# Down projection: the last two k-tiles as a third pair of seven half-size products

## Chip, cores and metric

The kernel runs on one core of a Trainium2 chip. The metric is the device time of one execution in microseconds (us), the median of several runs. The profile is that of one execution.

## What is computed

One decoder layer on 512 tokens of width 1024, in fp32: an RMSNorm, a combined projection, two token mixers (block-sparse attention and a chunkwise mLSTM) merged by gates, an output projection, then the feed-forward block and a last norm. The change lies in the feed-forward block:

```python
u = rms_norm(h, norm_ffn_g[l])
g, up = jnp.split(u @ w_gate_up[l], 2, axis=-1)     # 1024 -> 2 x 2816
h = h + (jax.nn.silu(g) * up) @ w_down[l]           # 2816 -> 1024
...
return rms_norm(h, norm_final_g)
```

2816 is 22 k-tiles of 128 rows for the down projection.

## The kernel before

Every operand of a matmul is split into a high and a low part (ScalarE copies the high part into a rounded type, VectorE subtracts it for the low part), and a product is three passes: high x high, high x low, low x high. Most products are done by a scheme of seven half-size products in place of eight (W11, S1, S2, W12, S3, S4, W22): sums of halves of the weights and of the activations are formed first, and the seven results are added up with signs. S1 is W21+W22, S2 is S1+W11, S3 is W11+W21, S4 is S2+W12.

The feed-forward block has 22 gate/up items ("gu", one per k-tile of the down projection, each seven products of 128x256 matmuls, `prod`, L1120 to L1122), and five groups of the down projection ("ds"). A group takes four k-tiles as two pairs. Each of its seven products is done for two token tiles of 128, 512 columns wide, and adds up over the two pairs (`ds_prod`, L1378 to L1380: six matmuls). A pair's operands come from an even and an odd gate/up item: `gu_last` keeps the even one's results and combines them with the odd one's.

Groups 0 to 3 add their results to the stored residual by accumulating DMAs on GpSimd's queue (L1395). The last group, `ds_end`, adds to the residual in SBUF (tiles h, loaded by `end_load`, L1615; `add_`, L1462), squares it on ScalarE, forms the reciprocal root on two engines (`rstd`, L1474 to L1477, and `refine`, L1483 and L1484), scales by it and by the final norm's weights g3, and issues the output DMAs on SP's and ScalarE's queues.

5 x 4 k-tiles are 20 of the 22. Before, the last two are multiplied directly: `gu_last` splits their activations (L1341 to L1345), `dl_prep` splits their weights, 1024 columns each (`raw`, loaded at L1091), and `last` (L1508 to L1510) multiplies them in three passes, in banks that it shares with the seven products where it can: 48 matmuls in units of 512 columns.

The order of the work on an engine is set by a priority: `plan` gives each product a due time on a clock of TensorE's work, `at(key, product, offset)` sets the priority of what is issued next to such a time plus an offset, and a list scheduler issues the lowest that is ready. `behind` and `issue_after` add an order without a semaphore. Weights are split at due time minus H_OFF (high) and L_OFF (low), sums at minus S_OFF.

Elsewhere, and early in the kernel, four stores of rows (scr<-rr, L1762) and half of the loads of stacked keys (ks<-sd, L475) are issued on GpSimd's queue.

Of the kernel before, what the change touches and what calls it, by code (L numbers as in the profile page):

```python
# [15 lines left out]
P = 128  # L16
# [61 lines left out]
H_OFF, L_OFF, S_OFF, U_OFF, E_OFF, O_OFF, D_OFF, S4_OFF, R_OFF, RD_OFF = 1800, 800, 3800, 0, 3000, 1500, 1500, 10000, 1440, 1360  # L78

# [23 lines left out]
def hybrid_layer_kernel(ctx: ExitStack, tc, xw, xT, xtm, wall, wgt, wwo, wgu, wds, wdl, g3v, vecs, wgates, consts, rope, out):  # L103
# [349 lines left out]
    def rope_group(kind, g):  # L453
# [18 lines left out]
        for key, parts in lay:  # L472
            stk = slot4(F32R, key)
            for e, i in enumerate(parts):
                (nc.gpsimd if e % 2 else nc.sync).dma_start(  # L475
                    f(stk[32 * e : 32 * e + 32]), sd[i].rearrange("(h r) t -> r h t", h=4)
                )
            for j in range(4):
                stacks[(key, 4 * g + j)] = stk[:, j, :]
# [525 lines left out]
    def plan():  # L1005

        t = 0
        LONG = {"W12": 4, "LAST": 1, "W22": 4, "S4": 5}
        i0, i1, i2 = ITEMS[:3]
        seq = [(WO_ITEM, w) for w in WO_W] + [(i0, "W11"), (i0, "S1"), (i1, "W11"), (i1, "S1")]  # L1010
        seq += [(i, w) for i in (i0, i1) for w in ("S2", "S4", "S3")]
        seq += [(i0, "W12"), (i0, "W22"), (i2, "W11"), (i1, "W12"), (i1, "W22")]
        for j, x in enumerate(ITEMS):
            if j < 2:
                continue
            if j == len(ITEMS) - 1:
# [66 lines left out]
    def ds_load(n):  # L1083
        g = sw["ds", n] = {"w": {}}
        for j, k in enumerate(("W11", "W21", "W22", "W12")):
            g[k] = blk(name="raw", raw=True)
            nc.sync.dma_start(g[k], wds[n, j])
        if n == NG - 1:
            for k in range(LK):
                raw["dl", k] = blk(name="raw", raw=True)  # L1090
                nc.sync.dma_start(raw["dl", k], wdl[k])  # L1091

    DS_W = ("W11", "S1", "S2", "W12", "S3", "S4", "W22")

    def ds_prep(n):
# [3 lines left out]
        for k in DS_W if n < NG - 1 else DS_W[:3] + (0, 1) + DS_W[3:5] + DS_W[:4:-1]:  # L1099
            if k in (0, 1):  # L1100
                dl_prep(k)
                continue
            if k[0] == "S":
# [3 lines left out]
                V.tensor_tensor(g[k], g[a], g[b], op=ALU.add)  # L1107
# [4 lines left out]
            V.tensor_tensor(w[k][1], g[k], f(w[k][0]), op=ALU.subtract)
# [209 lines left out]
    hid = []  # L1322

    def gu_last(i):
# [14 lines left out]
        if i >= 4 * NG:  # L1339

            V.tensor_tensor(u[:, A_], u[:, A_], t[:, A_], op=ALU.mult)  # L1341
            V.scalar_tensor_tensor(u[:, B_], u[:, B_], -1.0, t[:, B_], op0=ALU.mult, op1=ALU.mult)
            h, l = slot(F32R, "ach"), slot(F32R, "acl")
            c = act_(h, u, AF.Copy)
            V.tensor_tensor(l, u, f(h), op=ALU.subtract)  # L1345
            hid.append((h, l))
            if i == FT - 1:
                ph["ins"].append(raw_ins(c))
        elif i % 2 == 0:
# [5 lines left out]
        else:  # L1355
# [10 lines left out]
            split_hl(e[:, A_], dst=(q[:, A_], q[:, B_]))  # L1366
# [4 lines left out]
    def ds_prod(ps, w, n, o, t, first=False):  # L1371

        wh, wl = w
        c = slice(t * P, (t + 1) * P)
        for k in range(2):
            bh, bl = (x[:, c] for x in hb[n][k][o])
            d = slice(k * S, (k + 1) * S)
            T.matmul(ps, bh, wh[:, d], start=first and k == 0, stop=False, skip_group_check=not first)  # L1378
            T.matmul(ps, bh, wl[:, d], start=False, stop=False, skip_group_check=not first)  # L1379
            T.matmul(ps, bl, wh[:, d], start=False, stop=k == 1, skip_group_check=not first)  # L1380

    LK = FT - 4 * NG
    DL = []

    def dl_prep(k):
        at(ITEMS[-1], "W12", -H_OFF)
        DL.append(split_hl(raw.pop(("dl", k)), dst=(blk(F32R, "w"), blk(F32R, "w"))))

# [57 lines left out]
    def ds_end():  # L1446
# [3 lines left out]
        key = ("ds", n)  # L1450
        w = sw.pop(key)["w"]
# [4 lines left out]
        U = 1360  # L1456
        v_ = lambda: small([P, 1], "v1")
# [29 lines left out]
        def apply(t, q, j):  # L1487

            V.scalar_tensor_tensor(hs[t][j], hs[t][j], q, g3[j], op0=ALU.mult, op1=ALU.mult)
            act_(hs[t][1 - j], hs[t][1 - j], AF.Copy, scale=q)  # L1490
            for e in (j, 1 - j):
                nc.sync.dma_start(out[t][:, e * S : e * S + S], hs[t][e])

        def scale_out(t, q, j):

            act_(hs[t][j], hs[t][j], AF.Copy, scale=q)
            nc.sync.dma_start(out[t][:, j * S : j * S + S], hs[t][j])

        def times_g(t, j):
            V.tensor_tensor(hs[t][j], hs[t][j], g3[j], op=ALU.mult)  # L1500

        def last(ps, t, j, first=False, d=slice(0, S)):

            q, c = slice(t * P, (t + 1) * P), slice(j * S + d.start, j * S + d.stop)
            for k in range(LK):
                (ah, al), (wh, wl) = hid[k], DL[k]
                g = dict(skip_group_check=not first)
                T.matmul(ps[:, d], ah[:, q], wh[:, c], start=first and k == 0, stop=False, **g)  # L1508
                T.matmul(ps[:, d], ah[:, q], wl[:, c], start=False, stop=False, **g)
                T.matmul(ps[:, d], al[:, q], wh[:, c], start=False, stop=k == LK - 1, **g)  # L1510
# [29 lines left out]
        for t in two:  # L1540
            at(key, "W22", U * t - 1000)
            add_(t + 2, 1, Z[t], r[t + 2])
        at(key, "LAST")
        y = accb()
        last(y, 2, 1, first=True)
        at(key, "W22", 2000)
        add_(2, 1, y, nr[2])
        square(2, 1)
        for t in two:
            at(key, "W22", 2 * U * t)  # L1550
            ds_prod(X[t], w["W22"], n, 6, t)
            last(X[t], t, 1)
            at(key, "W22", 2 * U * t + 1000)
            times_g(t, 0)
            at(key, "W22", 2 * U * (t + 1) + 200)
# [19 lines left out]
        with tc.issue_after(raw_ins(i[1])):
            apply(1, qs[1], 1)
        y = accb()
        lo, hi = slice(0, HS), slice(HS, S)
        at(key, "S4", 2 * U)
        ds_prod(Z[1], w["S4"], n, 3, 1)  # L1580
        last(Z[1], 3, 0)
        at(key, "S4", 4 * U + 200)
        add_(3, 0, Z[1], nr[3])
        square(3, 0)
        nc.gpsimd.tensor_tensor(hs[3][0], hs[3][0], g3[0], op=ALU.mult)
        at(key, "S4", 4 * U)
        last(y, 3, 1, first=True, d=lo)
        at(key, "S4", 9 * U // 2 + 200)
        add_(3, 1, y, nr[3], lo)
        square(3, 1, lo)  # L1590
        at(key, "S4", 9 * U // 2)
        y = mmb()
        last(y, 3, 1, first=True, d=hi)
        at(key, "S4", 5 * U + 200)
        add_(3, 1, y, nr[3], hi)
        square(3, 1, hi)
        q, v, i = rstd(3, "S4", 5 * U + 800)
        with tc.issue_after(raw_ins(i[1])):
            scale_out(2, qs[2], 0)
        q = refine(q, v)  # L1600
        for d in (lo, hi):
            act_(hs[3][0][:, d], hs[3][0][:, d], AF.Copy, scale=q)
            V.scalar_tensor_tensor(hs[3][1][:, d], hs[3][1][:, d], q, g3[1][:, d], op0=ALU.mult, op1=ALU.mult)
            nc.sync.dma_start(out[3][:, S + d.start : S + d.stop], hs[3][1][:, d])
        nc.scalar.dma_start(out[3][:, 0:S], hs[3][0])
# [130 lines left out]
    def gates():  # L1736
# [24 lines left out]
        for b in range(4):  # L1761
            nc.gpsimd.dma_start(scr[:, RS[b]], rr[b])  # L1762
# [440 lines left out]
```

## Time and profile before

| | |
|---|---|
| median of 3 runs | 722.72 us (722.56 to 723.15) |
| profiled execution | 722.84 us |
| its span | 721.1 us |
| granted TensorE clock | 0.998 |
| TensorE busy | 712.7 us, 99% of the span, 4310 matmuls |
| VectorE busy | 642.4 us, 89% |
| ScalarE busy | 467.0 us, 65% |
| GpSimd busy | 82.8 us, 11% |

The profile names engines PE (TensorE; PEld its weight loads), DVE (VectorE), ACT (ScalarE), POOL (GpSimd) and SP (the queue that issues most DMAs; SPq and ACTq rows are DMA issues). A group or timeline row reads: start, duration, engine, line, operation, out<-in, partitions x elements, count, and in brackets the engine's idle time before it and what ended it. Matmuls overlap in the pipeline, so a matmul's duration is longer than the time until the next one starts.

### The profile page before, as it was taken

Reading aid. Unit: us, or ns where it says so; the run is one execution under the profiler, and the core shown is the slowest. Engines: PE = TensorE matmul, PEld = TensorE weight load, DVE = VectorE, ACT = ScalarE, POOL = GpSimd, SP = SyncE. Lnnn points to the kernel's source line nnn. Section 1 sums busy time; section 2 is a strip of 40 time slices with the busy share of each in tenths; the row PEclk is TensorE's granted clock in tenths of the full one; section 3 lists DMA queues with packets and bytes.
Section 4 is the critical chain, followed back from the end, with each engine's and each line's share of the span. In section 5 each row is a group of like instructions: output and inputs, shape, how many; then the busy total and the mean of one; then the engine's idle time right before and its main releaser. Section 6 shows DMA issues by size and latency. Waiting matters only on the chain.

```text
span 721.1 us, 11772 instructions
## 1 busy us (share of the span) xinstructions
PE 712.7 (99%) x4310; PEld 636.8 (88%) x4310; DVE 642.4 (89%) x1125; ACT 467.0 (65%) x822; POOL 82.8 (11%) x105
## 2 busy tenths in 40 slices
PE   9999999999999999999999999999999999999995
PEld 6888888888888889998889998999899899899984
DVE  7998876899986698999999998899899899989996
ACT  7535777678776666965679666566565665655555
POOL 0004010102011010100000001300300310220000
PEclk9999999999999999999999999999999999999999
DMA  9778563858385967766797355974985795696403
GB/s 335 261 225 230 191 204 108 215 226 219 111 230 119 313 139 179 207 202 205 200 308 193 117 162 132 246 208 143 206 251 130 187 266 167 154 243 207 152 0 118
DMA packets 57418, 138.95 MB, mean 193 GB/s; under 512 B 5884, under 2 KB 10500, under 8 KB 57232
## 3 DMA queue, kind: packets, MB, share of 16 engines
q1 hardware_dynamic: 40448, 100.78, 40.9%
q0 software_dynamic: 15472, 34.92, 26.4%
q10 hardware_dynamic: 1440, 2.49, 0.9%
q8 instruction: 34, 0.56, 0.3%
q14 instruction: 24, 0.20, 0.1%
HBM read 121.35 MB, written 29.66 MB: 209 GB/s over the span
## 4 chain that ended last, share of the span: by engine, by line
PE 97%; ACT 1%; DVE 1%; issue 1%; DMA 0%
PE mm L234 9%; PE mm L235 9%; PE mm L236 9%; PE mm L1120 6%; PE mm L1121 6%; PE mm L1122 6%; PE s L1120 3%; PE s L1122 3%; PE s L1121 3%; PE mm L1378 3%; PE mm L1379 3%; PE mm L1380 3%; PE mm L329 2%; PE acc L1880 2%; PE mm L521 2%; PE mm L522 2%
## 5 line engine op out<-in xcount | busy, mean ns | idle before, releaser
L1120 PE MATMUL mm<-bq,w 128*128 128x256 f32 x264 | 75.2, 285 | 0.0
L1121 PE MATMUL mm<-bq,w 128*128 128x256 f32 x264 | 74.9, 284 | 0.0
L1122 PE MATMUL mm<-bq,w 128*128 128x256 f32 x264 | 74.7, 283 | 0.0
L166 ACT ACTIVATE w<-raw 128x1024 fp32r<-128x1024 f32 (+1 forms) x62 | 60.4, 983 | 13.6 <-PE mm L235 4.7
L166 ACT ACTIVATE w<-s 128x1024 fp32r<-128x1024 f32 (+1 forms) x54 | 55.4, 1026 | 14.2 <-DVE s L725 4.6
L179 DVE TENSOR_TENSOR wl<-raw,wh 128x1024 fp32r<-128x1024 f32 x42 | 50.8, 1220 | 11.2 <-ACT wh L166 7.8
L166 ACT ACTIVATE wh<-raw 128x1024 fp32r<-128x1024 f32 x42 | 44.2, 1057 | 25.4 <-PE mm L235 21.5
L1067 DVE TENSOR_TENSOR w<-s,w 128x1024 fp32r<-128x1024 f32 x42 | 51.2, 1219 | 7.1 <-ACT w L166 7.1
L1120 PEld LDWEIGHTS mm<-bq,w 128*128 128x128 f32 x264 | 50.5, 191 | 0.5 <-ACT s L166 0.3
L1121 PEld LDWEIGHTS mm<-bq,w 128*128 128x128 f32 x264 | 50.5, 191 | 0.0
L1122 PEld LDWEIGHTS mm<-bq,w 128*128 128x128 f32 x264 | 50.5, 191 | 0.0
L1120 PE MATMUL s<-bq,w 128*128 128x256 f32 x176 | 49.9, 284 | 0.0
L1121 PE MATMUL s<-bq,w 128*128 128x256 f32 x176 | 49.7, 283 | 0.0
L1122 PE MATMUL s<-bq,w 128*128 128x256 f32 x176 | 49.7, 283 | 0.0
L993 POOL DMA_DIRECT2D s<-in_wgu_dram x19 | 16.7, 879 | 231.2 <-DVE acl L179 93.5
L234 PE MATMUL mm<-u,wh 128*128 128x512 f32 x104 | 40.9, 393 | 0.0
L236 PE MATMUL mm<-u,wh 128*128 128x512 f32 x104 | 40.7, 391 | 0.0
L235 PE MATMUL mm<-u,wl 128*128 128x512 f32 x104 | 40.7, 391 | 0.0
L236 PE MATMUL mm<-ul,wh 128*128 128x512 f32 x104 | 40.5, 389 | 0.0
L234 PE MATMUL mm<-uh,wh 128*128 128x512 f32 x104 | 40.5, 389 | 0.0
L235 PE MATMUL mm<-uh,wl 128*128 128x512 f32 x104 | 40.5, 389 | 0.0
L166 ACT ACTIVATE s<-mm 128x256 f32<-128x256 f32 x44 | 16.7, 380 | 29.2 <-PE mm L1122 29.2
(499 smaller groups left out, 2438.2 us busy)
## 6 DMA issues: line engine op xcount, KB each, us to landing
raw<-in_wall_dram SPq DMA_DIRECT2D x42, 512.0 KB, 4.5
raw<-in_wgu_dram SPq DMA_DIRECT2D x22, 512.0 KB, 4.7
raw<-in_wds_dram SPq DMA_DIRECT2D x20, 512.0 KB, 6.2
s<-in_wgu_dram SPq DMA_DIRECT2D x19, 512.0 KB, 4.9
s<-in_wgu_dram POOLq DMA_DIRECT2D x19, 512.0 KB, 5.6
w<-in_wgu_dram SPq DMA_DIRECT2D x22, 256.0 KB, 5.6
ws<-in_wwo_dram POOLq DMA_DIRECT2D x8, 512.0 KB, 8.9
raw<-ws SPq DMA_DIRECT2D x8, 512.0 KB, 4.3
```

The costliest lines, as they stand in the source:

```text
L166: return A.activation(out_, in_, func, **kw)
L179: V.tensor_tensor(l, src, f(h), op=ALU.subtract)
L234: T.matmul(ps, wh[:, c], rh[j], start=start and j == 0, stop=False)
L235: T.matmul(ps, wl[:, c], rh[j], start=False, stop=False)
L236: i = T.matmul(ps, wh[:, c], rl[j], start=False, stop=stop and j == n - 1)
L1067: V.tensor_tensor(dst[1], src, f(dst[0]), op=ALU.subtract)
L1120: T.matmul(ps, wh[:, c], bh, start=first and k == 0, stop=False, skip_group_check=not first)
L1121: T.matmul(ps, wl[:, c], bh, start=False, stop=False, skip_group_check=not first)
L1122: i = T.matmul(ps, wh[:, c], bl, start=False, stop=k == 3, skip_group_check=not first)
L1378: T.matmul(ps, bh, wh[:, d], start=first and k == 0, stop=False, skip_group_check=not first)
L1379: T.matmul(ps, bh, wl[:, d], start=False, stop=False, skip_group_check=not first)
L1380: T.matmul(ps, bl, wh[:, d], start=False, stop=k == 1, skip_group_check=not first)
```

## The change

The last two k-tiles become a third pair of the last group. Items 20 and 21 go through the even and odd path that the others use. The weights of the pair are taken in halves of 512 columns: `end_first` splits W11, `end_second` forms S3, S1 and S2 and splits S1, `end_rest` splits the rest and forms S4. These four sums are on GpSimd, and so are the low parts of S3, W22 and S4 (`POOL_LO`). The sum and the low part of S4 of the first two pairs (1024 columns) go from VectorE to GpSimd as well.

In `ds_end` each product now adds up over three pairs (nine matmuls of 512 columns). S1 and S4 of the second token tile are issued in two halves of 256 columns, in banks of their own. `last`, `dl_prep`, `apply`, `scale_out` and `times_g` are gone. The multiplications by g3 of four tiles and the scalings of three tiles are on GpSimd, those of the other halves on VectorE and, for one, on ScalarE. The small tiles of the norm get buffers of their own.

One more edit is early in the kernel: the four stores scr<-rr are ordered after the last load of ks on GpSimd's queue.

The core of the diff:

```diff
-        for k in DS_W if n < NG - 1 else DS_W[:3] + (0, 1) + DS_W[3:5] + DS_W[:4:-1]:
-            if k in (0, 1):
-                dl_prep(k)
-                continue
+        for k in DS_W if n < NG - 1 else DS_W[:5] + DS_W[:4:-1]:
...
-                V.tensor_tensor(g[k], g[a], g[b], op=ALU.add)
+                pool(n, k).tensor_tensor(g[k], g[a], g[b], op=ALU.add)
...
+POOL_LO = ('S3', 'W22', 'S4')
+    pool = lambda n, k: nc.gpsimd if n == NG - 1 and k == 'S4' else V
+    def end_sum(s, a, b, dst):
+        at(ITEMS[-1], s, -SE_OFF)
+        end[s] = dst
+        nc.gpsimd.tensor_tensor(dst, end[a], end[b], op=ALU.add)
+    def end_split(k, h, l):
+        at(ITEMS[-1], k, -H_OFF)
+        act_(h, end[k], AF.Copy)
+        at(ITEMS[-1], k, -L_OFF)
+        (nc.gpsimd if k in POOL_LO else V).tensor_tensor(l, end[k], f(h), op=ALU.subtract)
+        sw[ITEMS[-1]]["w"][k].append((h, l))
...
-            hb[i // 4].append(ops + [(q[:, A_], q[:, B_])])
+            hb[min(i // 4, NG - 1)].append(ops + [(q[:, A_], q[:, B_])])
...
-        for k in range(2):
+        for k, (wh, wl) in enumerate(w):
...
+        def scale_p(t, q, j):
+            nc.gpsimd.tensor_scalar(hs[t][j], hs[t][j], q, None, op0=ALU.mult)
+            nc.sync.dma_start(out[t][:, j * S : j * S + S], hs[t][j])
...
-            last(y, t, 0, first=True)
-            ds_prod(y, w["W12"], n, 2, t)
+            ds_prod(y, w["W12"], n, 2, t, first=True)
...
+            nc.gpsimd.tensor_tensor(hs[t][0], hs[t][0], g3[0], op=ALU.mult)
...
-        for b in range(4):
-            nc.gpsimd.dma_start(scr[:, RS[b]], rr[b])
+        with tc.issue_after(marks["stack"]):
+            for b in range(4):
+                nc.gpsimd.dma_start(scr[:, RS[b]], rr[b])
```

What this moves, row by row. GpSimd's last rows before (s and c tiles are results of the group before; h is the residual, g the final norm's weights):

```order
L1395 DMA h1d<-c_7165 128x512
L993 DMA s_7203<-in_wgu_dram 128x1024
L1585 ISA
L1585 TENSOR_TENSOR h_7700<-h_7700,g_7692 128x512
```

and after (raw_7349 and raw_7351 are the two tiles of the third pair's weights, sw_7602, sw_7622 sums of the first two pairs' weights, v the factors of the norm):

```order
L998 DMA s_7203<-in_wgu_dram 128x1024
L1105 ISA
L1105 TENSOR_TENSOR sw_7859<-raw_7349 128x512
L1105 TENSOR_TENSOR raw_7349<-raw_7349,raw_7351 128x512
L1105 TENSOR_TENSOR raw_7349<-raw_7349 128x512
L1111 TENSOR_TENSOR w_7870<-sw_7859,w_7870 128x512
L1111 TENSOR_TENSOR w_7870<-raw_7351,w_7870 128x512
L1105 TENSOR_TENSOR raw_7351<-raw_7349,raw_7351 128x512
L1111 TENSOR_TENSOR w_7875<-raw_7351,w_7875 128x512
L1144 TENSOR_TENSOR sw_7622<-sw_7602,raw_7347 128x1024
L1150 TENSOR_TENSOR w_7625<-sw_7622,w_7624 128x1024
L1554 TENSOR_TENSOR h_7690<-h_7690,g_7688 128x512
```

Three more multiplications by g and three scalings follow. Nine operations on weights now stand ahead of the first multiplication by g, in the order in which their inputs come.

VectorE around the end of the last gate/up item, before (gt and up are its two results, acl the low part of the operand):

```order
L1337 TENSOR_TENSOR gt_7787<-mm_7712,rb_4349 128x256
L179 TENSOR_TENSOR w_7609<-raw_7349,w_7608 128x1024
L179 TENSOR_TENSOR w_7613<-raw_7351,w_7612 128x1024
L1341 TENSOR_TENSOR up_7802<-up_7802,gt_7787 128x256
L1342 SCALAR_TENSOR_TENSOR up_7802<-up_7802,gt_7787 128x256
L1112 TENSOR_TENSOR w_7617<-raw_7347,w_7616 128x1024
L1345 TENSOR_TENSOR acl_7848<-up_7802,ach_7847 128x512
```

and after:

```order
L1376 TENSOR_TENSOR gt_7784<-mm_7708,rb_4349 128x256
L1111 TENSOR_TENSOR w_7865<-raw_7349,w_7865 128x512
L1150 TENSOR_TENSOR w_7609<-raw_7347,w_7608 128x1024
L1387 SCALAR_TENSOR_TENSOR up_7799<-up_7799,gt_7784 128x256
L1388 TENSOR_TENSOR up_7799<-up_7799,gt_7784 128x256
L1390 TENSOR_TENSOR gt_7658<-gt_7658,up_7799 128x256
L1391 SCALAR_TENSOR_TENSOR gt_7658<-up_7799,up_7673 128x256
L1111 TENSOR_TENSOR w_7865<-raw_7351,w_7865 128x512
L182 TENSOR_TENSOR acl_7845<-up_7799,ach_7844 128x512
L1393 TENSOR_TENSOR up_7673<-up_7799,gt_7658 128x256
L182 TENSOR_TENSOR acl_7851<-gt_7658,ach_7850 128x512
```

Four operations of 256 columns and one more low part of 512 come in between the gate multiplication and the end of the operands; gt_7658 and up_7673 belong to item 20. The low part of 1024 columns that stays there is another's (W12).

On TensorE, where the third pair's operand acl_7851 is first read, after (product S2 of both token tiles; w_7865 holds the third pair's S2 weights, w_7604 and w_7605 those of the first two pairs):

```order
L1409 MATMUL mm_7879<-w_7865,ach_7850 128x512
L1410 MATMUL mm_7879<-w_7865,ach_7850 128x512
L1409 MATMUL mm_7880<-w_7604,ach_7315 128x512
L1411 MATMUL mm_7879<-w_7865,acl_7851 128x512
L1410 MATMUL mm_7880<-w_7605,ach_7315 128x512
```

In before S2 ran over two pairs only. Here the third pair closes it, and a matmul of the other token tile is issued ahead of the one that reads the low part.

More of the change, by code (lines that the diff above doesn't have):

```diff
@@ L1007, in plan @@
         t = 0
-        LONG = {"W12": 4, "LAST": 1, "W22": 4, "S4": 5}
         i0, i1, i2 = ITEMS[:3]
@@ L1016, in plan @@
             if j == len(ITEMS) - 1:
-                seq += [(x, w) for w in ("S1", "S2", "W12", "S3", "LAST", "W22", "S4")]
+                seq += [(x, w) for w in ("S1", "S2", "W12", "S3", "W22", "S4")]
                 continue
@@ L1088, in ds_load @@
         if n == NG - 1:
-            for k in range(LK):
+            for k in range(2):
                 raw["dl", k] = blk(name="raw", raw=True)
@@ L1093, in hybrid_layer_kernel, with end_first, end_second, end_rest @@
     DS_W = ("W11", "S1", "S2", "W12", "S3", "S4", "W22")
+    end = {}
+    pool = lambda n, k: nc.gpsimd if n == NG - 1 and k == 'S4' else V
[9 more added lines that the diff above has]
+        sw[ITEMS[-1]]["w"][k].append((h, l))
+    def end_first():
+        Lo, Hi = slice(0, S), slice(S, D)
+        d0, d1 = (raw.pop(("dl", i)) for i in range(2))
+        end.update(W11=d0[:, Lo], W21=d0[:, Hi], W12=d1[:, Lo], W22=d1[:, Hi])
+        end_split("W11", slot(F32R, "w"), slot(F32R, "w"))
+    def end_second():
+        t = slot4(F32R, "w")
+        end_sum("S3", "W11", "W21", slot4(name="sw")[:, 0, :])
+        end_sum("S1", "W21", "W22", end["W21"])
+        end_sum("S2", "S1", "W11", end["W11"])
+        end_split("S1", t[:, 0, :], t[:, 1, :])
+    def end_rest():
+        for i, k in enumerate(("S2", "W12", "S3", "W22", "S4")):
+            if i % 2 == 0:
+                t = slot4(F32R, "w")
+            if k == "S4":
+                end_sum("S4", "S2", "W12", end["W12"])
+            end_split(k, t[:, 2 * (i % 2), :], t[:, 2 * (i % 2) + 1, :])
     def ds_prep(n):
@@ L1338, in gu_last @@
         act_(t, t, AF.Silu)
[L1339 to L1349, printed above, removed]
+        if i % 2 == 0:
             at(key, "W22", O_OFF)
@@ L1365, in gu_last, with ds_prod @@
             q = slot(F32R, "ac")
-            split_hl(e[:, A_], dst=(q[:, A_], q[:, B_]))
+            c = act_(q[:, A_], e[:, A_], AF.Copy)
+            V.tensor_tensor(q[:, B_], e[:, A_], f(q[:, A_]), op=ALU.subtract)
+            if i == FT - 1:
+                ph["ins"].append(raw_ins(c))
             ops = [(p[0][:, c], p[1][:, c]) for p in (p0, p1, p2) for c in (A_, B_)]
-            hb[i // 4].append(ops + [(q[:, A_], q[:, B_])])
-    def ds_prod(ps, w, n, o, t, first=False):
-        wh, wl = w
+            hb[min(i // 4, NG - 1)].append(ops + [(q[:, A_], q[:, B_])])
+    def ds_prod(ps, w, n, o, t, first=False, d=slice(0, S)):
         c = slice(t * P, (t + 1) * P)
-        for k in range(2):
+        for k, (wh, wl) in enumerate(w):
             bh, bl = (x[:, c] for x in hb[n][k][o])
[L1377 to L1387, printed above, removed]
+            g = dict(skip_group_check=not first)
+            T.matmul(ps, bh, wh[:, d], start=first and k == 0, stop=False, **g)
+            T.matmul(ps, bh, wl[:, d], start=False, stop=False, **g)
+            T.matmul(ps, bl, wh[:, d], start=False, stop=k == len(w) - 1, **g)
     def ds_run(n):
@@ L1450, in ds_end @@
         key = ("ds", n)
+        marks["end0"], marks["end"] = st["S3"], st["W22"]
+        with behind("end0"):
+            end_second()
+        with behind("end"):
+            end_rest()
         w = sw.pop(key)["w"]
@@ L1455, in ds_end @@
         ss = {}
-        U = 1360
-        v_ = lambda: small([P, 1], "v1")
+        U = 2040
+        v_ = lambda: sm.tile([P, 1], F32, name=nm("v1"), tag="end", bufs=24)
         def add_(t, j, ps, c, d=slice(0, S)):
@@ L1485, in refine, with scale_g @@
             return r
-        def apply(t, q, j):
+        def scale_p(t, q, j):
+            nc.gpsimd.tensor_scalar(hs[t][j], hs[t][j], q, None, op0=ALU.mult)
+            nc.sync.dma_start(out[t][:, j * S : j * S + S], hs[t][j])
+        def scale_g(t, q, j):
             V.scalar_tensor_tensor(hs[t][j], hs[t][j], q, g3[j], op0=ALU.mult, op1=ALU.mult)
[L1490 to L1496, printed above, removed]
-            nc.sync.dma_start(out[t][:, j * S : j * S + S], hs[t][j])
[L1499 to L1510, printed above, removed]
+            nc.sync.dma_start(out[t][:, j * S : j * S + S], hs[t][j])
         qs = []
         X, Z = [mmb() for t in two], [sb() for t in two]
+        lo, hi = slice(0, HS), slice(HS, S)
+        zh = sb()
         for t in two:
@@ L1541, in ds_end @@
             at(key, "W22", U * t - 1000)
[L1542 to L1548, printed above, removed]
+            for z, d in ((Z[t], slice(0, S)),) if t == 0 else ((Z[t], lo), (zh, hi)):
+                add_(t + 2, 1, z, r[t + 2], d)
+            square(t + 2, 1)
+            nc.gpsimd.tensor_tensor(hs[t + 2][1], hs[t + 2][1], g3[1], op=ALU.mult)
         for t in two:
-            at(key, "W22", 2 * U * t)
+            at(key, "W22", U * t)
@@ L1551, in ds_end @@
             ds_prod(X[t], w["W22"], n, 6, t)
[L1552 to L1555, printed above, removed]
+            at(key, "W22", U * (t + 1) + 200)
             add_(t, 1, X[t], r[t])
             square(t, 1)
-            q, v, _ = rstd(t, "W22", 2 * U * (t + 1) + 2000)
+            q, v, i = rstd(t, "W22", U * (t + 1) + 1600)
             qs.append(refine(q, v))
-            if t == 0:
-                apply(0, qs[0], 1)
+            scale_p(t, qs[t], 0)
@@ L1575, in ds_end @@
[L1575 to L1599, printed above, removed]
+        at(key, "S4", U)
+        ds_prod(Z[1][:, lo], w["S4"], n, 3, 1, d=lo)
+        at(key, "S4", 3 * U // 2 + 200)
+        add_(3, 0, Z[1], nr[3], lo)
@@ L1600, in ds_end @@
+        square(3, 0, lo)
+        at(key, "S4", 3 * U // 2)
+        ds_prod(zh[:, hi], w["S4"], n, 3, 1, d=hi)
+        at(key, "S4", 2 * U + 200)
+        add_(3, 0, zh, nr[3], hi)
+        square(3, 0, hi)
+        at(key, "S4", 2 * U + 400)
+        scale_p(2, qs[2], 1)
+        q, v, i = rstd(3, "S4", 2 * U + 800)
+        with tc.issue_after(raw_ins(i[0])):
+            scale_g(2, qs[2], 0)
         q = refine(q, v)
         for d in (lo, hi):
-            act_(hs[3][0][:, d], hs[3][0][:, d], AF.Copy, scale=q)
```

46 lines of the change are left out of this document (26 added, 20 removed).

## The prediction, made before the result was known

> **What bounds the kernel now.** I read the page's busy shares and its chain first, then the windows of the last 80 us, then the timelines of TensorE, VectorE and the queues at the end.
>
> ```profile
> PE 712.7 (99%) x4310; PEld 636.8 (88%) x4310; DVE 642.4 (89%) x1125; ACT 467.0 (65%) x822; POOL 82.8 (11%) x105
> PE 97%; ACT 1%; DVE 1%; issue 1%; DMA 0%
> ```
>
> The first row gives busy time per engine, the second the chain that ended last: TensorE is nearly the whole of it. The windows (columns: PE, PEld, DVE, ACT and POOL busy, granted clock, DMA share, GB/s) place that in the stretch of the change:
>
> ```profile
> 660.00:680.00 20.00, 20.00 (x158) 19.35 (x156) 18.50 (x32) 11.42 (x19) 0.00 (x0) 1.00 0.54 185
> 680.00:700.00 20.00, 20.00 (x111) 17.37 (x111) 18.76 (x25) 11.28 (x17) 0.00 (x0) 1.00 0.00 1
> 700.00:722.00 22.00, 13.85 (x67) 11.43 (x65) 15.11 (x36) 10.82 (x29) 1.26 (x1) 0.93 0.26 96
> ```
>
> PE is busy all 20 us of both windows, so a matmul less is time less. VectorE is second, at 18.5 and 18.8 of 20: it has 1.2 to 1.5 us to spare per window. GpSimd does nothing there.
>
> TensorE's timeline gives the matmul prices (start, duration, engine, line):
>
> ```profile
> 677.52 0.40 PE L1378 MATMUL mm<-w,ach 128*128 128x512 f32 x1
> ...
> 686.58 0.40 PE L1379 MATMUL s<-w,ach 128*128 128x512 f32 x1
> ...
> 712.26 0.28 PE L1508 MATMUL acc<-w,ach 128*128 128x256 f32 x1
> ...
> 713.58 0.28 PE L1510 MATMUL mm<-w,acl 128*128 128x256 f32 x1
> ```
>
> Durations overlap, so I price by starts. From 686.58 to 712.26 lie 113 matmuls of 512 columns: 25.68/113 = 0.227 us each. From 712.26 to 713.58 lie 11 steps of 256 columns: 0.12 each. The last one starts at 713.58; the span ends at 721.1, 7.5 us later, and the profiled run took 722.84, 1.74 us more than its span. That run is 0.12 above the median of 722.72.
>
> **The change: TensorE.** From 677.52, the first product of the last group, before issues 126 matmuls of 512 columns (84 of the seven products, 42 of the direct ones), 12 of 256 at the end, and 48 of 256 of the last gate/up item: 126 x 0.2273 + 60 x 0.12 = 35.84; the rows give 713.70 - 677.52 = 36.18, so some 0.3 us are gaps. After: 7 products x 2 token tiles x 9 matmuls = 126 in units of 512, of which the second tiles of S1 and S4 (18) are issued as 36 halves. That is 108 x 0.2273 + 36 x 0.12 + 48 x 0.12 = 34.63. Gain 1.2 us: 6 matmuls saved are 1.36, the extra halving costs 0.15. The matmuls would end at about 712.5.
>
> **VectorE, where the slack is none.** The third pair needs the two activations combined and split, more work than before. Its prices:
>
> ```profile
> 675.93 1.23 DVE L1112 TENSOR_TENSOR w<-raw,w 128x1024 fp32r<-128x1024 f32 x1 [0.55 <-ACT w L166]
> ...
> 686.81 0.42 DVE L1337 TENSOR_TENSOR gt<-mm,rb 128x256 f32<-128x256 f32 x1
> 687.14 2.35 DVE L179 TENSOR_TENSOR w<-raw,w 128x1024 fp32r<-128x1024 f32 x2
> 689.41 0.42 DVE L1341 TENSOR_TENSOR up<-up,gt 128x256 f32<-128x256 f32 x1
> 689.75 0.42 DVE L1342 SCALAR_TENSOR_TENSOR up<-up,gt 128x256 f32<-128x256 f32 x1
> 690.08 1.22 DVE L1112 TENSOR_TENSOR w<-raw,w 128x1024 fp32r<-128x1024 f32 x1
> 691.22 0.68 DVE L1345 TENSOR_TENSOR acl<-up,ach 128x512 fp32r<-128x512 f32 x1
> 691.82 1.40 DVE L1462 SCALAR_TENSOR_TENSOR h<-mm,nrc,h 128x512 f32<-128x512 f32 x2
> 693.14 1.22 DVE L1107 TENSOR_TENSOR sw<-raw,raw 128x1024 f32<-128x1024 f32 x1
> ```
>
> From start to start: 256 columns 0.34, 512 columns 0.60, 1024 columns 1.14, a 512 addition from PSUM 0.66. In after, the last gate/up item's W22 ends 19 matmuls of 512 and 49 of 256 past 677.52, at 688.0 (before: 13 and 48). The gate multiplication then starts 0.25 later, as it did before; up to the low part of the third pair's operand for S2 (acl_7851) VectorE runs six 256 steps, four 512 and one 1024: 6 x 0.34 + 4 x 0.60 + 1.14 = 5.6, so it lands at about 693.9. TensorE reaches the first matmul that reads it 17 of 512 and 17 of 256 after W22, 5.9 us, at 693.9. Zero slack. The other tight point is the low half of the first product's weights (w_7593), ready in before at 677.07 (675.93 + 1.14) for 677.52; the added sum and operand work of item 20 ahead of it delays it by about 0.6. I allow 0 to 0.4 for both, and take 0.1.
>
> **GpSimd.** Four sums and three low parts of 512, one sum and one low part of 1024, four multiplications by g3 and three scalings of 512 are put on it. Its only price in the trace:
>
> ```profile
> 664.48 6.54 SPq L1091 DMA_DIRECT2D raw<-in_wdl_dram  x2
> ...
> 714.15 1.26 POOL L1585 TENSOR_TENSOR h<-h,g 128x512 f32<-128x512 f32 x1 [64.53 <-ACT sq L166]
> raw<-in_wdl_dram SPq DMA_DIRECT2D x2, 512.0 KB, 3.8
> ```
>
> 1.26 for 512, twice VectorE's 0.60; 1024 columns are 2.5 by doubling. Between 672 and 702 that is 7 x 1.26 + 2 x 2.5 = 13.8 us in 30: room enough. The raw weights are issued by 671.0 and landed by 674.8; S3, S1 and S2 need 3.8 us in turn from about 672 and are due on TensorE after 689. The first sum waits for the landing, and all of GpSimd's rows stand behind it, the longest string last: the S4 sum of the third pair, then the sum and low part of pairs 0 and 1 (2.5 each), ScalarE between them: done by 701.5, TensorE reads S4 at about 708, slack 6 us. GpSimd's own speed is thus covered; what is not covered is what it does to VectorE (rival B). Moving this work off VectorE also takes two 1024 operations (2.3 us) and one 512 multiplication from it before 711.
>
> **The tail.**
>
> ```profile
> 713.89 0.48 DVE L1462 SCALAR_TENSOR_TENSOR h<-mm,nrc,h 128x256 f32<-128x256 f32 x1 [0.19 <-PE mm L1510]
> 714.50 0.21 DVE L1474 TENSOR_SCALAR v<-v,v 128x1 f32<-128x1 f32 x1
> 715.01 0.21 DVE L1477 TENSOR_SCALAR v<-v,v 128x1 f32<-128x1 f32 x1 [0.30 <-ACT sq L166]
> ...
> 716.03 0.88 DVE L1603 SCALAR_TENSOR_TENSOR h<-h,v,g 128x256 f32<-128x256 f32 x2
> 715.45 1.54 ACT L166 ACTIVATE h<-h,v 128x512 f32<-128x512 f32 x3
> 717.02 0.36 ACTq L1605 DMA_DIRECT2D out_dram<-h  x1
> 716.61 0.88 SPq L1604 DMA_DIRECT2D out_dram<-h  x2
> out_dram<-h SPq DMA_DIRECT2D x2, 128.0 KB, 2.4
> ```
>
> From the last matmul's start to the last output issue (about 717.1) 3.5 us pass, then 4.0 to the span's end. The form stays: last half added, squared, root, refined, scaled in halves by VectorE and ScalarE, three issues. New is the queue of outputs: SP now also holds the tile that GpSimd scales last (h_7695). Its factor is ready at about 713.2; its scaling is a one-input form that the trace doesn't have, between VectorE's 0.60 and GpSimd's 1.26. I take 1.26, the row of its own engine: 714.5. The last row's scaling comes at 714.8, so the queue isn't held. The tail keeps its 7.5 us, give or take 0.2. The Trainium skill, "GPSIMD Engine Reference", section 4.1, says that one-input operations run at about line rate there: an estimate of 0.6 by that, with the output free at 713.8 and no case left for rival C below; no run here shows it.
>
> **The early edit.** Two pairs of ks loads now go ahead of the first of the four scr stores on GpSimd's queue:
>
> ```profile
> 54.76 0.54 POOL L1762 DMA_DIRECT2D scr<-rr  x1 [7.93 <-DVE rr L1757]
> 55.28 2.18 POOL L475 DMA_DIRECT2D ks<-sd  x4
> 57.45 0.53 POOL L1762 DMA_DIRECT2D scr<-rr  x1
> ...
> 64.64 0.39 PE L523 MATMUL acc<-wh,ul 128*128 128x512 f32 x1
> 64.86 0.22 PE L1788 MATMUL s<-ks,qs 128*128 128x128 f32 x1
> ```
>
> The loads start 0.5 us sooner, the first store 2.2 later. TensorE reached ks at 64.86 without a gap (0.22 after its last start), so nothing is won; the other stores are not issued before 57.45 either. Zero, bounds -0.3 and +0.3 (a store's 0.5 either way).
>
> **Sum.** -1.2 (matmuls) + 0.1 (tight points) + 0 (tail, GpSimd, early edit) = -1.1 to -1.2. Against the run's 722.84 that is 721.65; against the median, 721.5. The bound of faster and slower is 0.2%, 1.45 us, which this gain just misses.
>
> **Rivals.** A is the above, with VectorE undisturbed.
>
> B, slower: GpSimd and VectorE hold each other up when both read two SBUF tiles. In before GpSimd's one operation ran from 714.15 to 715.41 beside a PSUM addition (0.48, like others) and 128x1 operations, so nothing excludes it. Place: 688 to 694, where VectorE has no slack and GpSimd does the low parts of S3 and W22 and the S4 sum, 1.26 each. If VectorE stops for two or three, TensorE waits 2.5 to 3.8 for acl_7851; the sums from 672 on do the same ahead of w_7593, worth 0.7 to 1.8 beyond its slack. With -1.2 from the matmuls: +1.3 to +4.4, middle +2.3, 725.0. It decides from 1.2 us of VectorE standing still in that stretch, one operation. For it: VectorE is at 94%. Against it: some operations there are PSUM additions, and GpSimd may come second and be the one that waits, with 6 us to spare. The Trainium skill, "SBUF — State Buffer", section "Who interferes with whom", states such a rule: a VectorE instruction with two SBUF inputs contends with a GpSimd instruction that reads SBUF, and the second to issue fully blocks. By it B would be the forecast; no run here shows it yet.
>
> C: the gain is given back at the output queue. If GpSimd's scalings and multiplications are late by more than 0.3 us (the space between 714.5 and 714.8), SP's issues stand behind h_7695, in order. One more 1.26 in GpSimd's row costs 1.0: 722.5, no change.
>
> **Chances.** A 0.53: it holds at -1.2 plus or minus 0.7 (the tight points, the tail, the early edit), so 0.25 of it is beyond 1.45, where VectorE's relief also closes the gaps, and 0.28 within. B 0.35: 0.32 slower, 0.03 within. C 0.12: 0.11 within, 0.01 slower. Faster 0.25, same 0.42, slower 0.33. The range leaves out A's best (0.07) and the worse part of B (0.12): 720.7 to 725.5; the likeliest case alone is 720.8 to 722.2.
>
> **What would show it.** Right: PE without idle time from 677 to the end, the last matmul starting 1.2 us earlier, VectorE's 1024 operations still 1.14 apart while POOL works, the last output issue at about 715.9. B shows as longer VectorE rows beside POOL rows and a PE gap of over 1 us at the third pair's S2 or at the first product. C shows as an SP issue of h_7695 after the last row's scaling. I am wrong if PE ends earlier and the span doesn't, or if another stretch than this one moves by over 0.5 us.

## The result, and the profile after

The changed kernel takes 730.78 us (median of 4 runs, 730.52 to 731.48); before, run beside it, 722.87. The ratio is 1.0111, 95% interval 1.0094 to 1.0129: 8 us slower, outside the predicted range.

The page of the changed kernel (busy time, and the chain that ended last):

```profile
PE 712.9 (98%) x4316; PEld 635.7 (87%) x4316; DVE 650.7 (89%) x1127; ACT 467.3 (64%) x825; POOL 108.2 (15%) x120
PE 91%; DVE 5%; issue 2%; ACT 1%; DMA 1%; SPq 0%; DVEq 0%; ACTq 0%
```

VectorE is busy 8.3 us longer in all, TensorE is no longer busy throughout, and VectorE has 5% of the chain. The windows place it (PE, PEld, DVE, ACT, POOL busy, clock, DMA share, GB/s):

```profile
660.00:680.00 20.00, 18.64 (x154) 18.33 (x152) 19.25 (x29) 10.77 (x17) 4.54 (x3) 1.00 0.52 176
680.00:700.00 20.00, 17.02 (x104) 14.26 (x102) 19.48 (x29) 10.62 (x19) 4.94 (x4) 1.00 0.02 9
700.00:720.00 20.00, 18.49 (x86) 14.97 (x87) 18.58 (x27) 10.24 (x22) 13.56 (x9) 1.00 0.01 1
```

TensorE idles 1.4, 3.0 and 1.5 us where it idled nothing. TensorE's waits of over 1 us from 650 us on (engine and line, what it waited for, us in total, times, longest):

```profile
PE mm L1411 <- DVE acl L182: 1.5, 1, 1.5
PE mm L1409 <- ACT sq L169: 1.5, 1, 1.5
PE mm L1161 <- DVE gt L1351: 1.4, 1, 1.4
PE mm L1409 <- ACT ach L169: 1.2, 1, 1.2
```

The first row is the operand that the prediction found without slack. For the second the view names ScalarE's squaring of the residual, which itself follows VectorE's additions; the matmul also waits for its bank, which the VectorE addition from 711.30 to 712.03 empties. The third is item 20's W22, which waits for its bank until VectorE has emptied it at 677.16 (L1351); that operation stands behind the first two rows below. What VectorE did there, and GpSimd at the same time, from their timelines:

```profile
673.43 1.78 DVE L182 TENSOR_TENSOR acl<-gt,ach 128x512 fp32r<-128x512 f32 x1
675.13 1.51 DVE L1396 TENSOR_TENSOR ac<-up,ac 128x256 fp32r<-128x256 f32 x1
...
693.03 1.51 DVE L1387 SCALAR_TENSOR_TENSOR up<-up,gt 128x256 f32<-128x256 f32 x1
694.46 1.51 DVE L1388 TENSOR_TENSOR up<-up,gt 128x256 f32<-128x256 f32 x1
695.89 0.41 DVE L1390 TENSOR_TENSOR gt<-gt,up 128x256 f32<-128x256 f32 x1
...
697.76 1.49 DVE L1393 TENSOR_TENSOR up<-up,gt 128x256 f32<-128x256 f32 x1
...
702.01 2.63 DVE L1396 TENSOR_TENSOR ac<-up,ac 128x256 fp32r<-128x256 f32 x1
...
707.02 3.04 DVE L1150 TENSOR_TENSOR w<-raw,w 128x1024 fp32r<-128x1024 f32 x1
```

```profile
675.01 1.35 POOL L1105 TENSOR_TENSOR raw<-raw,raw 128x512 f32<-128x512 f32 x1 [0.35 <-DMA raw<-in_wdl_dram]
...
692.64 1.62 POOL L1111 TENSOR_TENSOR w<-sw,w 128x512 fp32r<-128x512 f32 x1 [13.97 <-ACT w L169]
694.21 1.47 POOL L1111 TENSOR_TENSOR w<-raw,w 128x512 fp32r<-128x512 f32 x1
...
697.37 1.60 POOL L1105 TENSOR_TENSOR raw<-raw,raw 128x512 f32<-128x512 f32 x1 [1.69 <-issue]
...
701.42 2.93 POOL L1144 TENSOR_TENSOR sw<-sw,raw 128x1024 f32<-128x1024 f32 x1 [0.42 <-PE mm L1410]
706.58 2.40 POOL L1150 TENSOR_TENSOR w<-sw,w 128x1024 fp32r<-128x1024 f32 x1 [2.22 <-DVE w L1150]
```

Read them side by side. The 256-column operations at 693.03 and 694.46 take 1.51 where the one at 695.89 takes 0.41: GpSimd's low parts run from 692.64 to 695.68. The one at 702.01 takes 2.63, beside GpSimd's 1024 sum; the low part at 707.02 takes 3.04 where before it took 1.22, beside GpSimd's. The one at 697.76, ahead of the operand that TensorE waits for, takes 1.49 beside the sum at 697.37. Each is longer by 1.1 beside a 512 operation and by 1.8 to 2.2 beside one of 1024.

The ends tell how long the hold lasts. VectorE's 256-column operations end 0.28 or 0.29 us after GpSimd's operation beside them (676.64 after 676.36, 694.54 after 694.26, 695.97 after 695.68, 699.25 after 698.97, 704.64 after 704.35), the one of 1024 ends 1.08 after it (710.06 after 708.98). That is a little less than such operations take from start to start (0.34 and 1.14). So in these rows VectorE gets through its data only when GpSimd has finished, and the hold is what GpSimd's operation still has to run.

TensorE's steps, and its last matmul (before: 713.58, with 7.5 us to the span's end):

```profile
677.63 0.39 PE L1161 MATMUL mm<-bq,w 128*128 128x256 f32 x1 [1.36 <-DVE gt L1351]
...
695.78 0.39 PE L1411 MATMUL mm<-w,acl 128*128 128x512 f32 x1
697.41 0.50 PE L1409 MATMUL mm<-w,ach 128*128 128x512 f32 x1 [1.25 <-ACT ach L169]
...
697.98 0.40 PE L1409 MATMUL mm<-w,ach 128*128 128x512 f32 x1
699.91 0.50 PE L1411 MATMUL mm<-w,acl 128*128 128x512 f32 x1 [1.53 <-DVE acl L182]
...
710.29 0.39 PE L1411 MATMUL mm<-w,acl 128*128 128x512 f32 x1
712.18 0.47 PE L1409 MATMUL mm<-w,ac 128*128 128x512 f32 x1 [1.51 <-ACT sq L169]
...
720.45 0.28 PE L1411 MATMUL s<-w,acl 128*128 128x256 f32 x1
```

Around 697, 700 and 712 three steps lose 1.40, 1.70 and 1.66 us against a step of 0.23. The end, on GpSimd, VectorE and SP:

```profile
722.10 2.05 POOL L1518 TENSOR_SCALAR h<-h,v 128x512 f32<-128x512 f32 x1 [0.67 <-DVE v L1503]
```

```profile
723.51 0.88 DVE L1600 SCALAR_TENSOR_TENSOR h<-h,v,g 128x256 f32<-128x256 f32 x2
```

```profile
724.17 0.33 SPq L1519 DMA_DIRECT2D out_dram<-h  x1
724.60 0.38 SPq L1524 DMA_DIRECT2D out_dram<-h  x1
725.07 1.51 SPq L1602 DMA_DIRECT2D out_dram<-h  x2
```

GpSimd's scaling takes 2.05, not 1.26. SP issues that tile at 724.17, another behind it, and the last row's two halves, scaled at 723.95 and 724.39, only from 725.07.

The 8.6 us between the two spans (the profiled execution of the changed kernel is the slowest of its four) can be split by marks that both traces have. The first mark is the SiLU of item 19, in before and after:

```profile
666.90 0.64 ACT L171 ACTIVATE gt<-gt 128x512 f32<-128x512 f32 x1 [1.63 <-DVE gt L1337]
```

```profile
667.64 0.64 ACT L174 ACTIVATE gt<-gt 128x512 f32<-128x512 f32 x1 [1.63 <-DVE gt L1376]
```

0.74 lies before it, in a part that the change does not touch but for the early edit, which is taken up below (in the twelve profiles of the layer here this mark stands between 666.67 and 667.64). From there to the last matmul's start it is 46.68 before and 52.81 after: 6.13. The tail is 7.52 and 9.25: 1.73. Of the 6.13, the matmuls that are saved give back 1.2, so that waits cost 7.3: 1.6 ahead of the last group's first product (679.88, 12.24 after the mark; before 10.62), most of it the 1.36 of item 20's W22; 0.4 at that product's second matmul, for the low half of its weights; 4.8 in the three steps above; the rest, 0.6, in small ones.

### The profile page after: what moved, and what is told of

Its sections match the earlier page's. It is cut to its first block, busy times and chain, and to the rows that moved or that the text cites. A ratio compares the mean times of both kernels' runs of the same rounds, so it can differ in the third digit from the quotient of the medians.

```text
span 729.7 us, 11822 instructions
## 1 busy us (share of the span) xinstructions
PE 712.9 (98%) x4316; PEld 635.7 (87%) x4316; DVE 650.7 (89%) x1127; ACT 467.3 (64%) x825; POOL 108.2 (15%) x120
## 4 chain that ended last, share of the span: by engine, by line
PE 91%; DVE 5%; issue 2%; ACT 1%; DMA 1%; SPq 0%; DVEq 0%; ACTq 0%
PE mm L237 9%; PE mm L238 8%; PE mm L239 8%; PE mm L1161 5%; PE mm L1162 5%; PE mm L1163 5%; PE s L1163 3%; PE s L1161 3%; PE s L1162 3%; PE mm L1410 2%; PE mm L1409 2%; PE mm L1411 2%; PE acc L1879 2%; PE mm L527 2%; PE mm L526 2%
```

## The experiments

The two measures of each profile are T, from item 19's SiLU to the last matmul's start, and E, from there to the span's end; they are from one execution of each kernel. Each ratio is to runs of before beside it (medians 722.87 to 723.35).

| kernel | time, us | ratio to before, 95% | T | E |
|---|---|---|---|---|
| before | 722.87 | | 46.68 | 7.52 |
| changed | 730.78 | 1.0094 to 1.0129 | 52.81 | 9.25 |
| e1 fills in place of arithmetic on weights | 723.67 | 0.9999 to 1.0018 | 45.56 | 9.23 |
| e2 weights on VectorE | 728.18 | 1.0052 to 1.0082 | 48.33 | 10.69 |
| e3 tail off GpSimd | 731.62 | 1.0105 to 1.0139 | 53.85 | 8.02 |
| e5 sums by DMA, rest on VectorE | 725.41 | 1.0022 to 1.0047 | 46.68 | 9.83 |
| e6 nothing on GpSimd | 726.67 | 1.0037 to 1.0064 | 47.92 | 9.58 |
| e7 fills, tail off GpSimd | 722.59 | 0.9985 to 1.0003 | 45.60 | 8.00 |
| e8 early edit alone | 723.33 | 0.9995 to 1.0013 | 46.68 | 7.54 |
| e9 e5 with the first additions by DMA | 722.54 | 0.9985 to 1.0003 | 45.77 | 7.90 |
| e10 two low parts on VectorE | 729.96 | 1.0084 to 1.0115 | 50.37 | 10.26 |
| e12 e9 with its tail reordered | 723.83 | 0.9996 to 1.0014 | 45.73 | 8.69 |

**e1, fills.** The theory after the result is the prediction's rival B, a hold of VectorE by GpSimd; its rival L is that VectorE's own work is too long.

```diff
-        nc.gpsimd.tensor_tensor(dst, end[a], end[b], op=ALU.add)
+        nc.gpsimd.memset(dst, 0.5)
...
-        (nc.gpsimd if k in POOL_LO else V).tensor_tensor(l, end[k], f(h), op=ALU.subtract)
+        if k in POOL_LO:
+            nc.gpsimd.memset(f(l), 0.0)
```

> The changed kernel with the nine operations of GpSimd on weights (four sums, three low parts, the sum and the low part of the first pairs' S4) replaced by fills of a constant into the same tiles: they write and read nothing, so these products are computed from constants. VectorE's work is unchanged. Theory B (a GpSimd operation that reads SBUF stops VectorE's operations with two SBUF inputs): the long VectorE rows are gone, TensorE's gaps at the first product, at S2 and at W22 (7.3 us in all) close to under 1 us, time about 724 (723.5 to 725.5), the rest above before being the tail. Rival L (VectorE's own row, longer by the third pair's operands, is what is late; GpSimd is not in it): the gaps stay, 729.5 to 731.

723.67, and TensorE waits nowhere from 600 us on. The first of the two operations that took 1.51:

```profile
690.56 0.42 DVE L1396 SCALAR_TENSOR_TENSOR up<-up,gt 128x256 f32<-128x256 f32 x1
```

T is 45.56, 1.12 less than before; the sum in the prediction said 1.2. So all of the 7.3 us of waits go with the arithmetic of GpSimd's nine operations. E is as in the changed kernel. The fills also wait for less than the arithmetic did, so this run alone does not tell a hold from a late result; the rows above and the probes do.

**e2, weights on VectorE** (`POOL_LO = ()`, the sums and S4 with `V.`).

> The changed kernel with those nine operations on VectorE, the tail as it is. Theory B: 6.5 us of work more on VectorE (7 x 0.60 + 2 x 1.14), but about 13 us of standing still less; some waits of TensorE stay, since VectorE has only 1 to 1.5 us to spare in 20: 725 to 728. Rival L: more work on the engine that is late makes it later: 733 or more.

728.18, just above the range, on the side of theory B: more work for VectorE is faster than having it stopped. T is 48.33: VectorE is full (below), E 10.69.

**e3, tail off GpSimd.**

```diff
-            nc.gpsimd.tensor_scalar(hs[t][j], hs[t][j], q, None, op0=ALU.mult)
+            act_(hs[t][j], hs[t][j], AF.Copy, scale=q)
...
-            nc.gpsimd.tensor_tensor(hs[t][0], hs[t][0], g3[0], op=ALU.mult)
+            V.tensor_tensor(hs[t][0], hs[t][0], g3[0], op=ALU.mult)
```

> The changed kernel with the four multiplications by g3 on VectorE and the three scalings on ScalarE, the weights on GpSimd as they are. Theory C (GpSimd's scalings, 1.8 to 2.0 us each, hold the outputs behind them on SP): from the last matmul to the span's end 7.5 us instead of 9.25, time 729.0. If the outputs do not wait for GpSimd: 730.8, no change.

The expectation is missed: 731.62, not to be told from the changed kernel. In the profile E does fall by 1.23, to 8.02, but T rises by 1.04. Not for a wait: the wait of W22 at 712 is gone. The profile shows another clock: 13 steps of TensorE from 699.58 to 705.13, of 512 columns each, take 0.43 us instead of 0.23, 2.6 us more in all, at a granted clock of 0.83 from 695 to 700 and 0.50 from 700 to 705. In the other eleven profiles of the layer it is 1.00 from 690 to 712, in the changed kernel too, behind the same two waits at S2. What lowered it stays open, and so does what the other executions of e3 lost (731.11 to 732.55, this one 730.38): the run says little of T.

**e4 and e11, probes.** Loops of operations of 512 columns and nothing else.

> Not the layer: rows of VectorE and GpSimd operations of 512 columns, first each engine alone, then together, and nothing else. Theory B: with two SBUF inputs on VectorE, four GpSimd operations with two inputs cost VectorE about 4 x 1.26 us more than alone; with one input from PSUM or with one input only they cost nothing; fills cost nothing. Rival L: VectorE's rows are as long beside GpSimd as alone (0.60 each), and GpSimd's may be longer. GpSimd's scaling by a column: 0.6 by the Trainium skill's page GPSIMD Engine Reference, 1.8 by the row of the changed kernel if nothing stood in its way there.

> Not the layer: 16 VectorE operations of 512 columns in four forms (two SBUF inputs; two SBUF inputs and a column; PSUM and SBUF; one SBUF input), each alone and then beside four GpSimd operations (two inputs; scaling by a column; copy; fill). Theory B, from the first probe: two-input forms lose what GpSimd's operation is busy (5.3 for the two-input one, about half of the 6.5 of the scaling), the PSUM form loses nothing beside any, and fills cost under 0.5. Rival: the fills cost as much per us as the others, as the 1.9 us in the first probe's row may say.

From the first, four GpSimd operations alone (two inputs, scaling by a column, copy):

```profile
26.66 5.28 POOL L143 TENSOR_TENSOR t<-t,t 128x512 f32<-128x512 f32 x4
...
32.84 6.54 POOL L144 TENSOR_SCALAR t<-t,q 128x512 f32<-128x512 f32 x4
...
40.26 2.64 POOL L147 COPY t<-t 128x512 f32<-128x512 f32 x4
```

The scaling costs 1.64 each, more than the two-input operation's 1.32. From the second, VectorE's 16 operations: two SBUF inputs alone, PSUM and SBUF alone, one SBUF input alone; then a small operation of two SBUF inputs and the 16 two-input operations behind it, both beside GpSimd's two-input operations; the 16 beside fills; the PSUM form and the one-input form beside the two-input operations:

```profile
13.01 11.58 DVE L139 TENSOR_TENSOR t<-t,t 128x512 f32<-128x512 f32 x16
...
38.43 12.53 DVE L141 SCALAR_TENSOR_TENSOR t<-pb,q,t 128x512 f32<-128x512 f32 x16
...
51.61 8.30 DVE L142 TENSOR_SCALAR t<-t,q 128x512 f32<-128x512 f32 x16
...
60.48 1.19 DVE L152 TENSOR_TENSOR s<-s 128x1 f32<-128x1 f32 x1 [0.37 <-POOL s L151]
61.59 14.40 DVE L139 TENSOR_TENSOR t<-t,t 128x512 f32<-128x512 f32 x16
...
103.85 11.59 DVE L139 TENSOR_TENSOR t<-t,t 128x512 f32<-128x512 f32 x16
...
175.95 12.52 DVE L141 SCALAR_TENSOR_TENSOR t<-pb,q,t 128x512 f32<-128x512 f32 x16
...
230.06 10.94 DVE L142 TENSOR_SCALAR t<-t,q 128x512 f32<-128x512 f32 x16
```

And from the first again, the 16 two-input operations beside GpSimd's four:

```profile
54.35 15.49 DVE L139 TENSOR_TENSOR t<-t,t 128x512 f32<-128x512 f32 x16
```

The hold is there without the layer: 11.58 becomes 14.40 beside four additions, and stays 11.59 beside fills; with one input in PSUM 12.53 stays 12.52. The 14.40 is not the whole loss. GpSimd's additions start at 60.39, and the small operation at 60.48 takes 1.19 where it takes 0.16 ahead of the other rows: another 1.0. In the first probe the additions start behind it, and the row itself is 15.49. Both ways VectorE loses 3.9 for four. The 1.9 us for fills that I read in the first probe came from a wrong comparison (0.60 each, the kernel's step, where this loop has 0.72 alone). The size was expected wrong: 3.9 us for four, 1.0 each, where I had 5.3; in the kernel it is 1.1 each. Four scalings by a column, 6.5 us alone, cost VectorE's two-input row only 1.5 (13.10), where about 3.3 were expected.

**e5, sums by DMA.** S1 and S3 by accumulating loads, the other sums by DMAs between tiles:

```diff
-        end[s] = dst
-        nc.gpsimd.tensor_tensor(dst, end[a], end[b], op=ALU.add)
+        end[s] = end[b]
+        nc.gpsimd.dma_start(end[b], end[a], accum_op=ALU.add)
```

with all low parts on VectorE and the tail as in e3.

> The changed kernel with no arithmetic on GpSimd at its end. The third pair's sums S1 and S3 come from accumulating loads, S2, S4 and the first pairs' S4 from accumulating DMAs between SBUF tiles; all low parts are on VectorE (2.9 us more than in the run with fills), multiplications by g3 on VectorE, scalings on ScalarE. Theory B: TensorE has no gap of over 0.3 us from 677 on and ends 1.2 us earlier than before, relative to the start of the last item; with the tail as before the time is 721.9 (721.4 to 722.8), 0.1% to 0.2% under before. Rival: VectorE is too full for it without GpSimd, TensorE waits for low parts: 723.5 to 726.

725.41: the rival's range. TensorE's one wait is of 0.8, for the bank of W22's product, and T is as before; E is 9.83: VectorE's row is late when the matmuls end, and the four chains of the norm come one behind the other.

**e6, nothing on GpSimd** (e2 and e3 together).

> The changed kernel with weights' sums, low parts and multiplications by g3 on VectorE and the scalings on ScalarE. Theory B with C: the run with the weights on VectorE lost 2 us on TensorE and 3 us in the tail to GpSimd's multiplications and scalings there; the latter come back, a VectorE that is full keeps the former: 725 (724 to 726.5). If GpSimd's tail cost nothing: 728.

726.67, 0.2 above the range. Its windows show the limit:

```profile
680.00:700.00 20.00, 20.00 (x121) 17.56 (x120) 19.81 (x34) 12.78 (x20) 0.00 (x0) 1.00 0.01 2
```

VectorE is busy 19.81 of 20. So rival L, dead as the cause of the 8 us, holds for the alternative: VectorE has no room for this work either.

**e7, fills with the tail off GpSimd.**

> The run with fills (weights' operations on GpSimd replaced by fills of a constant, so that these products are computed from constants), now with the multiplications by g3 on VectorE and the scalings on ScalarE. Theory C: the 9.2 us from the last matmul's start to the span's end become 7.6 to 8.0: 722.3 (721.9 to 722.8). If the outputs do not wait for GpSimd's scalings: 723.7 as with fills alone.

722.59, E 8.00 after 9.23. With VectorE free, taking the tail from GpSimd gives 1.2 us in the profile and 1.1 in the time.

**e8, the early edit alone**, on the kernel before.

> The kernel before with the early edit alone (the four stores of rows ordered after the loads of keys on GpSimd's queue). As predicted: no change, within 0.3 us of before. Rival: the 0.75 us by which the changed kernel's items 0 to 20 are late in its profile come from it: 0.5 to 1.0 slower.

723.33, ratio 1.0004: no change, as predicted.

**e9, first additions by DMA.** To e5:

```diff
+        def add_p(t, j, ps, c, d=slice(0, S)):
+            s = slot(name="pt")[:, d]
+            act_(s, ps[:, d], AF.Copy, scale=c)
+            nc.gpsimd.dma_start(hs[t][j][:, d], s, accum_op=ALU.add)
...
-            add_(t, 0, X[t], nr[t])
+            add_p(t, 0, X[t], nr[t])
```

> The run with the sums by DMA, and the first additions to the residual (results of W11, S1 and S2, seven operations of VectorE, 4 us) made by ScalarE (copy with the factor) and an accumulating DMA into the residual's tile. Theory: VectorE full of work is what is left of the loss once GpSimd no longer stops it; freed of 4 us, TensorE has no gap and the four chains of the norm start 3 us earlier: 7.6 us from the last matmul's start to the span's end, time 721.9 (721.4 to 722.8), 0.1% to 0.2% under before. Rival: the tail is late for another reason (the chains of the norm one behind the other): 724 or more.

From issue to landing, the DMAs that add 256 KB into the residual take 5.3 us, those that form sums of weights 4.5, 4.6 and 8.0. VectorE's rows beside them keep their lengths (0.42 for 256 columns, 0.68 for 512).

722.54, ratio 0.9994 (0.9985 to 1.0003): the whole layer, no wait of TensorE in the end, T 0.91 under before, E 0.38 above it. It takes back all that the change lost and is not to be told from before.

**e10, two low parts on VectorE** (`POOL_LO = ('S4',)`).

> The changed kernel with two of GpSimd's nine operations moved, the low parts of S3 and W22, to VectorE, where they come behind the operand that is late (acl of the third pair). Theory B: two holds of 1.1 us each ahead of that operand go, TensorE's two gaps around S2 (1.4 and 1.7 us) shrink by about 2 in all, 728.8 (728 to 729.8). Rival L: VectorE has 1.2 us more to do: 731 to 732.

729.96, outside the range and on B's side. The gaps at S2 are gone (3.1 us), and another stands at S3:

```profile
PE mm L1410 <- DVE w L1150: 2.8, 2, 2.6
```

Ahead of it GpSimd's sum of the third pair's S4 is itself stopped, by VectorE, whose four two-input operations from 693.99 on follow each other without a gap; the last of them, and the sum:

```profile
695.53 1.21 DVE L1144 TENSOR_TENSOR sw<-raw,raw 128x1024 f32<-128x1024 f32 x1
```

```profile
694.30 3.59 POOL L1105 TENSOR_TENSOR raw<-raw,raw 128x512 f32<-128x512 f32 x1 [16.60 <-ACT ach L169]
```

The sum ends at 697.89, 1.15 after VectorE's last. ScalarE has that sum to split ahead of the item's last operand (ac), for which VectorE then idles:

```profile
698.89 1.31 DVE L1396 TENSOR_TENSOR ac<-up,ac 128x256 fp32r<-128x256 f32 x1 [2.15 <-ACT ac L169]
```

T is still 2.4 shorter; E is 1.0 longer.

**e12, the tail reordered.**

> The run with the first additions by DMA, with two operations moved in its tail: VectorE's scaling of the second token tile (0.67 us) goes behind the last addition, and the scaling of one half of the third tile goes from ScalarE, where it stood ahead of the last logarithm, to VectorE. Theory: what is left in that tail (7.9 us against 7.5 before) is these operations ahead of the last row's chain; the tail gets 0.4 to 0.7 us shorter, 722.0 (721.5 to 722.4), just measurably under before. Rival: the chain is bound elsewhere: 722.5 as it was.

Missed: 723.83, E 8.69 instead of 7.90. The constant term of the last logarithm now stood behind the scaling that I had put on VectorE:

```profile
714.94 0.49 DVE L1610 TENSOR_SCALAR h<-h,v 128x512 f32<-128x512 f32 x1
715.35 0.21 DVE L1517 TENSOR_SCALAR v<-v,v 128x1 f32<-128x1 f32 x1
```

ScalarE waited 1.04 for it, until 715.65. No version here is measurably faster than before.

## Why the prediction was wrong

- **TensorE's sum was right.** Predicted -1.2 us from the count of matmuls; with nothing to wait for, T was 1.12 (e1), 1.08 (e7) and 0.91 (e9) shorter. The two tight points cost nothing there either: e1 has no wait of TensorE. (What the change puts ahead of w_7593 is the low part of W11, not work of item 20; its 0.6 is the size that was priced.)
- **The step that failed is "A is the above, with VectorE undisturbed", the forecast's choice of A over B.** The rows of before held nothing that excluded the hold, and VectorE had no slack where GpSimd would work. The Trainium skill, "SBUF — State Buffer", section "Who interferes with whom", states the rule; the chance of 0.35 for B was too low against it. The probes agree with the rule for two SBUF inputs (11.58 to 14.40), for a PSUM input (12.53 to 12.52) and for fills beside two inputs. "Fully blocks" fits GpSimd's two-input operations: in the kernel VectorE's held operations end 0.28 (256 columns) or 1.08 (1024) after GpSimd's, and in the probes four additions of 5.3 us cost VectorE 3.9. It does not fit its scalings, which cost 1.5 of 6.5.
- **B's own price was too small.** In the stretch it named, 2.5 to 3.8 were priced and 3.1 measured (1.40 + 1.70); and the sign that B named, a gap of over 1 us at the third pair's S2, is there. Ahead of the first product 0.7 to 1.8 were priced and 1.6 measured, but that near agreement is in part luck: the price was for w_7593, which cost 0.4 on top, and the 1.6 is mostly item 20's W22, whose bank the prediction did not look at. Left out were the two 1024 operations on GpSimd, whose cover I had called 6 us of slack: the slack was GpSimd's, and they held VectorE for about 2 us each, so that the bank of W22 came free 1.66 late. The sentence "some operations there are PSUM additions" was true and did not help, since these stand behind the held ones in VectorE's row.
- **C came with B, not instead of it.** I took the rivals as exclusive. The output queue did stand behind h_7695, because GpSimd's scaling costs 1.64 alone and 2.05 there, where I took 1.26; E rose by 1.73, and in e7 1.2 of it came back. The Trainium skill, "GPSIMD Engine Reference", section 4.1, has one-input operations at about line rate; the copy (2.64/4 = 0.66) agrees with that, the scaling by a column does not (1.64, VectorE's 8.30/16 = 0.52), and the measurement decides.
- **The early edit** was zero, as predicted (e8). The 0.74 before the first mark is not the change's: e10, which has the edit too, has the mark earliest of all, at 666.67.
- **What remains open:** which engine goes first is not derived. In the changed kernel GpSimd's low part got in between two of VectorE's operations (692.64), in e10 its sum stood through four of them. Nor are 0.6 of the 7.3 us of waits put to single steps, or the lower clock in e3's profile explained.

Without GpSimd the change would still not have paid on VectorE (e6, 726.67). The seven half-size products save six matmuls, 1.2 us of TensorE, and need sums and low parts in exchange, in the stretch where VectorE was at 94%. Only when sums and first additions went to DMAs and ScalarE (e9) did the saving appear in the whole layer, and the tail took part of it.

## What to carry to other kernels

Before moving work from VectorE to GpSimd, list which VectorE operations with two SBUF inputs will run beside it, and charge each two-input operation of GpSimd to VectorE's row too, at nearly its own length (1.0 to 1.1 of 1.3 us here); idle time of GpSimd is no room where VectorE is full. An accumulating DMA can make a sum of two tiles without stopping VectorE, if its landing (4.5 to 8.0 us here) can be waited for. Rivals that sit in different places add up: price them together.

## What the runs showed of the hardware

- GpSimd's scaling of 512 columns by a column of factors takes 1.64 us, slower than its two-input operation (1.32).
- Beside a two-input operation of GpSimd, a held VectorE operation with two SBUF inputs ends 0.28 us (256 columns) or 1.08 (1024) after it, so the hold is what GpSimd's operation still has to run. Scalings on GpSimd hold it for less (1.5 us for four of 6.5).
- The hold works both ways, and GpSimd can lose to more than one operation: a sum of 1.3 us took 3.59 behind four of VectorE's (e10).
- VectorE's one-input scaling from SBUF is held too (8.30 to 10.94 beside four GpSimd additions, 11.97 in the first probe), which I had expected to be free.
